# Second feed-forward product: seven block products over 14 of 22 row chunks instead of 12, with three plain chunks ahead instead of four

## The chip, the cores and the metric

The kernel runs on one core of a Trainium2 chip, as one program. The time is the device time of one execution in microseconds (us). The core's engines each work through a queue of their own: TensorE (PE, with its weight loads PEld), VectorE (DVE), ScalarE (ACT), GpSimd (POOL) and SyncE (SP), which here only issues DMAs. Semaphores make one wait for another.

## The reference

Two layers, each of a feed-forward block, a token mixer with three kinds of attention, and another feed-forward block, each with a residual and a layer norm. Four feed-forward blocks in all; the change lies in their second product, `h @ w2`:

```python
D_MODEL = 1024
SEQ = 512
D_FF = 2816

def _swiglu(x, w1, w2):
    gt, up = jnp.split(x @ w1, 2, axis=-1)
    return (jax.nn.silu(gt) * up) @ w2

    for l in range(DEPTH):
        x = _layer_norm(DN_ALPHA * x + 0.5 * _swiglu(x, ffn1_w1[l], ffn1_w2[l]), ln1_g[l], ln1_b[l])
        mix = _token_mix(x, ...)
        x = _layer_norm(DN_ALPHA * x + mix, ln2_g[l], ln2_b[l])
        x = _layer_norm(DN_ALPHA * x + 0.5 * _swiglu(x, ffn2_w1[l], ffn2_w2[l]), ln3_g[l], ln3_b[l])
```

## The kernel before

All matrices are float32 in memory. For TensorE each operand is split into a high part (`hi`, the value rounded to fp32r) and a low part (`lo`, the rest), and each product is made as three: hi x hi, lo x hi, hi x lo. ScalarE makes `hi` (L160 for weights, L434 for activations, L560 for the rows of h), VectorE makes `lo` (L161, L435, L561).

`h` has 2816 rows, 22 chunks of 128 (`KF`). It lies transposed in `ha` (chunks 0 to 17) and `hb` (the tail, 18 to 21, `NTAIL`). Its 512 columns are the tokens. `w2` is 22 chunks of 128 rows by 1024 columns. The result fills eight banks `accs[tb][hf]`: four blocks of 128 tokens, two halves of 512 columns. A plain chunk is 4 x 2 x 3 = 24 products of 128x128 by 128x512 (L195, `mm_rows`).

The order of one feed-forward block behind the first product (`ffn`, `short_rows`, `rows_ln`):

1. Ahead: the plain chunks of `LEAD` (12 to 15 before). While TensorE is in them, the operands of the next part are made.
2. The block part (`short_rows`, products at L453): chunks 0 to 11 (`2 * NW`, NW = 6) are taken as a 2 x 2 block matrix: tokens in halves H1 and H2, chunks in halves of NW, columns in halves of 512. Seven block products (Winograd's form of Strassen's scheme) stand in for eight. The names of the seven, in order of use: f_e (with differences of `bt` and `b1`), f_z (steps `z`), f_1 (with `b1`), f_6 (with `bt`), f_r (steps `r_`), f_7 (with `b1`) and f_4 (with `bt`). Each runs in steps `q` of two chunks: 2 x 2 x 3 = 12 products. `c11` to `c22` are the four quarters of the result in PSUM; `c21` serves as the scratch quarter, and `copies` (L459) and `add` (L464) carry what is shared between the seven.
3. Behind: chunks 16 and 17, plain, then the tail, token block by token block, with the layer norm.

The operands of the block part are made on the way. VectorE makes the block sums of h in `ha` (L477, L482, L483, L507), the differences of w2's quarters in `bt` and `b1` (L490, L497, L517, L537) and all low parts. The split activations lie in four sets of 2 x NW chunks: `xh`, `xl` (the input of the first product, done with by then) and two tiles `fs0`, `fs1`. f_e, f_1, f_z, f_6, f_7, f_r and f_4 take the sets 0, 1, 2, 3, 0, 1, 3. The split weights (`unit`) go round five pairs of buffers, so the split for one step waits for the products of the step five before.

`b1` and `bt` are loaded at the second chunk of `LEAD` (L428); the quarters for `z` and `r_` come through the ring of three `raw` buffers. In the first block of the first layer `b_parts` also paces 16 small loads of GpSimd, one behind each of the first 16 splits (L442, L443).

PE's and POOL's instructions are issued as written. Those of DVE, ACT and SP are put in order by the framework's planner when the program is built, by its own model of time; on the chip each engine then follows that order strictly, and `tc.issue_after` (`behind`) adds edges to it.

The tiles of the pool `stp` lie where the pool `w1p` of the first product was, and wait tile by tile for its last users; behind them the same place goes to `xa` and the tail's `hs` tiles.

Of the kernel before, what the change touches and what calls it, by code (L numbers as in the profile page):

```python
# [66 lines left out]
def body(tc, a, out, depth=DEPTH):  # L67
# [259 lines left out]
    NW = 6  # L327
    LEAD = range(2 * NW, KF - NTAIL - 2)
# [79 lines left out]
    def short_rows(st, w2, accs, hs, h_parts):  # L408
# [5 lines left out]
        pl.tile([P, 2, S], F32R, name="hs", tag="hs", bufs=2)  # L414
        ec, xc = ([pl.tile([P, S], F32, name=f"{n}{t}") for t in range(2)] for n in ("ec", "xc"))
        b1 = [pl.tile([P, KD, P], F32, name=f"b1{q}") for q in range(NW // 2)]
        sets = [x.rearrange("p a (b c) -> p (a b) c", b=2) for x in (xh, xl)]
        sets.append(pl.tile([P, 2 * NW, 256], F32R, name="fs0"))
        pl.tile([P, S], F32, name="uc", tag="uc", bufs=4)
        bt = [pl.tile([P, KD, P], F32, name=f"bt{q}") for q in range(NW // 2)]  # L420
        sets.append(pl.tile([P, 2 * NW, 256], F32R, name="fs1"))
# [4 lines left out]
        def rows(t, r, half, q):  # L426
            k0 = (r * NW + 2 * q) * P
            nc.sync.dma_start(t.rearrange("p (c k) f -> p c (k f)", c=2),  # L428
                              w2[k0:k0 + 2 * P, 512 * half:512 * half + 512].rearrange("(c p) f -> p c f", p=P))
            return t  # L430

        def a_parts(i, src):
            t = sets[i][:, 0:2 * NW]
            A.activation(t[:, 0:NW], src, AF.Copy)  # L434
            tt(t[:, NW:2 * NW], src, t[:, 0:NW].bitcast(F32), op=OP.subtract)  # L435
            return t

        def b_parts(raw):
            w = wsplit(raw)
# [6 lines left out]
        def prod(o, x, w, q, first=False):  # L446
            hi, lo = w
            xh_, xl_ = x[:, 0:NW], x[:, NW:2 * NW]
            for t in range(2):
                for j in range(2):  # L450
                    k, c, s = 2 * q + j, slice(4 * j, 4 * j + 4), slice(t * P, t * P + P)
# [4 lines left out]
        def copies(o, n=None):  # L456
            d = n or [pl.tile([P, S], F32, name="uc", tag="uc", bufs=4) for _ in range(2)]
            for t in range(2):
                A.activation(d[t], o[t], AF.Copy)  # L459
            return d  # L460
# [5 lines left out]
        Q = range(NW // 2)  # L466

        for n, k in enumerate(LEAD):
            if k not in hs:
                h_parts(k, pl.tile([P, 2, S], F32R, name="hs", tag="hs", bufs=2))  # L470
            w = wrows(w2, k)
            if n == 1:
                for q in Q:
                    rows(b1[q], 0, 0, q)
                    rows(bt[q], 0, 1, q)
                with behind(st.last):
                    tt(a21, a21, a22, op=OP.add)  # L477
                    f_e = a_parts(0, a21)
            if n == 2:
                with behind(st.last):  # L480
                    f_1 = a_parts(1, a11)
                    tt(a21, a21, a11, op=OP.subtract)  # L482
                    tt(a11, a12, a21, op=OP.subtract)  # L483
                    f_z = a_parts(2, a11)
# [3 lines left out]

        for q in Q:
            tt(bt[q], bt[q], b1[q], op=OP.subtract)  # L490
            prod(c21, f_e, b_parts(bt[q]), q, q == 0)
        copies(c21, ec)

        def z(q):
            r = rows(wraw(), 1, 1, q)
            prod(c12, f_z, b_parts(r), q)
            tt(bt[q], r, bt[q], op=OP.subtract)  # L497

        z(0)
        f_6 = a_parts(3, a21)  # L500
        for q in Q:
            prod(c21, f_1, b_parts(b1[q]), q, q == 0)
# [5 lines left out]
        f_7 = a_parts(0, a21)  # L508
        for q in Q:
            prod(c21, f_6, b_parts(bt[q]), q)  # L510
            if q == 0:
                z(2)
        u = copies(c21)
        f_r = a_parts(1, a12)
        f_4 = a_parts(3, a22)
        for q in Q:
            tt(b1[q], bt[q], b1[q], op=OP.subtract)  # L517
        h_parts(LEAD[-1] + 1, st.lnp.tile([P, 2, S], F32R, name="hs", tag="t2"))
        w = {}

        def r_(q):
            r = rows(wraw(), 1, 0, q)
            w[q] = r
            prod(c11, f_r, b_parts(r), q)

# [4 lines left out]
        for q in Q:  # L530
            prod(c21, f_7, b_parts(b1[q]), q)
        u = copies(c21)
        add(c21, xc)
        for q in Q:
            if q < 2:
                r_(q + 1)
            tt(bt[q], w[q], bt[q], op=OP.subtract)  # L537
            prod(c21, f_4, b_parts(bt[q]), q)
# [1147 lines left out]
```

## Time and profile before

| | |
|---|---|
| runs | 2430.63, 2430.72, 2431.18 us; median 2430.72 |
| profiled execution | 2430.75 us, of which the span of instructions 2428.7 |
| busy | PE 2417.4 us (100%), PEld 2178.8, DVE 1945.4 (80%), ACT 1235.0 (51%), POOL 264.4 (11%) |
| DMA | 286.29 MB, mean 118 GB/s |
| granted TensorE clock | 0.999 |

The chain is the sequence of work that ended last, followed back from the last instruction. A row of a timeline reads: start, duration, engine, line, operation, output<-inputs, shape, count, and in brackets the idle time just before it and what ended it. Buffer numbers are left out of names, so `bt` stands for each of the three `bt` tiles. Matmuls are pipelined: the duration of one (389 ns) is longer than the distance from one to the next.

### The profile page before, as it was taken

To read this page: it belongs to the slowest core of one execution; us is meant where nothing else is said; L and a number is where in the kernel's file an instruction comes from. 1 tells how busy PE (TensorE), PEld (TensorE's weight loads), DVE (VectorE), ACT (ScalarE), POOL (GpSimd) and SP (SyncE) were. 2 spreads that over 40 slices of the span, in tenths; PEclk is the share of its full clock that TensorE was granted. 3 is DMA by queue.
4 is the path that set the end of the run, shared out by engine and by line. 5 is a ranking of instruction groups with operands and counts; after the bars stand their busy time and mean duration, and the time that the engine had idled before them with its cause. 6 is when DMAs were issued, how large, how long until landed. Compare 5 with 4: busy or idle time off the path is not lost.

```text
span 2428.7 us, 42375 instructions
## 1 busy us (share of the span) xinstructions
PE 2417.4 (100%) x16257; PEld 2178.8 (90%) x16257; DVE 1945.4 (80%) x3786; ACT 1235.0 (51%) x2273; POOL 264.4 (11%) x472
## 2 busy tenths in 40 slices
PE   9999999999999999999999999999999999999998
PEld 9999888888889899998899998878888898999986
DVE  7997975687688689988789979666777886899795
ACT  4454544577644435445445445355766444445452
POOL 2000511133300000000000000122332000000000
PEclk9999999999999999999999999999999999999999
DMA  6332563533134433332533332645321344333233
GB/s 203 106 110 86 162 210 119 158 92 88 45 104 131 134 104 110 113 105 104 165 108 115 109 124 85 189 138 140 100 76 57 101 139 145 91 105 111 90 115 128
DMA packets 382699, 286.29 MB, mean 118 GB/s; under 512 B 17512, under 2 KB 347640, under 8 KB 382496
## 3 DMA queue, kind: packets, MB, share of 16 engines
q1 hardware_dynamic: 375024, 258.68, 35.9%
q0 software_dynamic: 7472, 24.90, 3.0%
q8 instruction: 128, 2.10, 0.4%
q14 instruction: 75, 0.61, 0.1%
HBM read 256.22 MB, written 17.88 MB: 113 GB/s over the span
## 4 chain that ended last, share of the span: by engine, by line
PE 99%; DMA 0%; DVE 0%; POOL 0%; SPq 0%; issue 0%; POOLq 0%; ACT 0%; DVEq 0%
PE pg L373 22%; PE acc L195 13%; PE pu L373 11%; PE acc L453 9%; PE pj L181 6%; PE pj L183 6%; PE pj L182 6%; PE pv L373 5%; PE brp L182 2%; PE brp L181 2%; PE brp L183 2%; PE sN L1081 2%; PE ptN L1123 1%; PE po L1142 1%; PE po L1029 1%; PE sF L1002 1%
## 5 line engine op out<-in xcount | busy, mean ns | idle before, releaser
L161 DVE TENSOR_TENSOR lo<-raw,hi 128x1024 fp32r<-128x1024 f32 x280 | 342.2, 1225 | 121.6 <-ACT hi L160 121.3
L160 ACT ACTIVATE hi<-raw 128x1024 fp32r<-128x1024 f32 x280 | 294.5, 1055 | 228.5 <-PE pg L373 56.9
L373 PE MATMUL pg<-xh,lo 128*128 128x256 f32 x1104 | 312.4, 283 | 0.0
L373 PE MATMUL pg<-xl,hi 128*128 128x256 f32 x1104 | 312.4, 283 | 0.0
L373 PE MATMUL pg<-xh,hi 128*128 128x256 f32 x1104 | 312.3, 283 | 0.0
L181 PE MATMUL pj<-xh,hi 128*128 128x512 f32 (+1 forms) x720 | 267.2, 371 | 0.5 <-ACT hi L1512 0.5
L355 ACT ACTIVATE hi<-ws 128x1024 fp32r<-128x1024 f32 x184 | 191.6, 1055 | 128.3 <-DVE ws L351 63.3
L183 PE MATMUL pj<-xh,lo 128*128 128x512 f32 (+1 forms) x720 | 254.6, 354 | 0.0
L182 PE MATMUL pj<-xl,hi 128*128 128x512 f32 (+1 forms) x720 | 254.4, 353 | 0.0
L356 DVE TENSOR_TENSOR lo<-ws,hi 128x1024 fp32r<-128x1024 f32 x184 | 223.4, 1221 | 38.3 <-ACT hi L355 37.5
L373 PEld LDWEIGHTS pg<-xh,hi 128*128 128x128 f32 x1104 | 211.9, 192 | 0.8
L373 PEld LDWEIGHTS pg<-xl,hi 128*128 128x128 f32 x1104 | 211.9, 192 | 0.8
L373 PEld LDWEIGHTS pg<-xh,lo 128*128 128x128 f32 x1104 | 211.9, 192 | 0.0
L373 PE MATMUL pu<-th,hi 128*128 128x256 f32 x608 | 172.1, 283 | 0.0
L373 PE MATMUL pu<-tl,hi 128*128 128x256 f32 x608 | 172.1, 283 | 0.0
L373 PE MATMUL pu<-th,lo 128*128 128x256 f32 x608 | 172.1, 283 | 0.0
L195 PE MATMUL acc<-hi,hs 128*128 128x512 f32 x512 | 158.2, 390 | 0.0
L183 PEld LDWEIGHTS pj<-xh,lo 128*128 128x128 f32 x720 | 136.1, 189 | 19.9 <-DVE lo L1513 0.2
L181 PEld LDWEIGHTS pj<-xh,hi 128*128 128x128 f32 x720 | 136.4, 189 | 15.5 <-issue 3.1
L358 ACT ACTIVATE dh<-raw 128x512 fp32r<-128x512 f32 x92 | 58.0, 631 | 177.5 <-PE pv L373 116.6
L182 PEld LDWEIGHTS pj<-xl,hi 128*128 128x128 f32 x720 | 136.8, 190 | 11.5 <-DVE xl L1598 0.2
L373 PEld LDWEIGHTS pu<-th,hi 128*128 128x128 f32 x608 | 116.7, 192 | 0.0
(394 smaller groups left out, 6501.5 us busy)
## 6 DMA issues: line engine op xcount, KB each, us to landing
raw<-in_ffn_w_dram SPq DMA_DIRECT2D x240, 512.0 KB, 3.8
raw<-in_w_in_dram SPq DMA_DIRECT2D x56, 512.0 KB, 3.8
raw<-in_w_gate_dram SPq DMA_DIRECT2D x48, 512.0 KB, 3.8
x_sp<-xa POOLq DMA_DIRECT2D x24, 512.0 KB, 5.8
ks<-hl SPq DMA_DIRECT2D x96, 128.0 KB, 2.3
xa<-x_sp POOLq DMA_DIRECT2D x16, 512.0 KB, 7.0
raw<-in_w_out_dram SPq DMA_DIRECT2D x16, 512.0 KB, 3.6
b<-in_ffn_w_dram SPq DMA_DIRECT2D x12, 512.0 KB, 7.6
```

The costliest lines, as they stand in the source:

```text
L160: nc.scalar.activation(hi[:, c], raw[:, c], AF.Copy)
L161: nc.vector.tensor_tensor(lo[:, c], raw[:, c], hi[:, c].bitcast(F32), op=OP.subtract)
L181: nc.tensor.matmul(o, hi[:, k], vh, start=first, stop=False)
L182: nc.tensor.matmul(o, hi[:, k], vl, start=False, stop=False)
L183: nc.tensor.matmul(o, lo[:, k], vh, start=False, stop=last)
L195: nc.tensor.matmul(o, x(k)[:, t], y[:, c], start=first and i == 0, stop=last and i == 2, skip_group_check=True)
L355: pa = nc.scalar.activation(hi, x, AF.Copy)
L356: pv = tt(lo, x, hi.bitcast(F32), op=OP.subtract)
L358: nc.scalar.activation(ud[0], ru[:, h2], AF.Copy)
L373: nc.tensor.matmul(o, wx, vx, start=first and k == 0 and i == 0, stop=k == 3 and i == 2, skip_group_check=True)
L453: nc.tensor.matmul(o[t], u[:, k, s], v[:, c], start=first and j == 0 and i == 0, stop=False, skip_group_check=True)
L1081: nc.tensor.matmul(o[:, 0:nb].rearrange("p k b j -> p (k b j)"), q, kx[:, 2 * b0:2 * (b0 + nb)].rearrange("p a b -> p (a b)"), start=i == ...
```

## The change

NW becomes 7: chunks 0 to 13 go through the seven block products. Each product has 7 chunks and runs in four steps, three pairs and a single (`Q`); loads, splits and differences of the single step are half as large. `LEAD` becomes chunks 14, 15 and 16; behind the block part stands chunk 17 alone. The steps `z` and `r_` become four each and are spread over the loops. For room, `hs` in the pool falls from two buffers to one, `uc` from four to two, and the four sets are taken strictly in turn (f_4 now in set 2, so behind f_z rather than f_6); the two tiles of sets lie directly behind `b1` and `bt`.

The core of the diff:

```diff
         return pts
 
     NTAIL = 4
-    NW = 6
-    LEAD = range(2 * NW, KF - NTAIL - 2)
+    NW = 7
+    LEAD = range(2 * NW, KF - NTAIL - 1)
     PLAIN = (0, 1, 2)
 
     def ffn_first(w1):
@@ -411,32 +411,38 @@
 
         V, A, tt = nc.vector, nc.scalar, nc.vector.tensor_tensor
         pl = pool("stp", side="right", reuse_waits="tile")
-        pl.tile([P, 2, S], F32R, name="hs", tag="hs", bufs=2)
+        pl.tile([P, 2, S], F32R, name="hs", tag="hs")
         ec, xc = ([pl.tile([P, S], F32, name=f"{n}{t}") for t in range(2)] for n in ("ec", "xc"))
-        b1 = [pl.tile([P, KD, P], F32, name=f"b1{q}") for q in range(NW // 2)]
-        sets = [x.rearrange("p a (b c) -> p (a b) c", b=2) for x in (xh, xl)]
-        sets.append(pl.tile([P, 2 * NW, 256], F32R, name="fs0"))
-        pl.tile([P, S], F32, name="uc", tag="uc", bufs=4)
-        bt = [pl.tile([P, KD, P], F32, name=f"bt{q}") for q in range(NW // 2)]
-        sets.append(pl.tile([P, 2 * NW, 256], F32R, name="fs1"))
+        pl.tile([P, S], F32, name="uc", tag="uc", bufs=2)
+        Q = [range(q, min(q + 2, NW)) for q in range(0, NW, 2)]
+        b1, bt = [], []
+        for x, n in ((b1, "b1"), (bt, "bt")):
+            x += [pl.tile([P, 4 * len(q), P], F32, name=f"{n}{q[0]}") for q in Q]
+            pl.tile([P, 2 * NW, 256], F32R, name=f"fs{n}", tag=f"fs{n}")
+        sets = [x.rearrange("p a (b c) -> p (a b) c", b=2)[:, 0:2 * NW] for x in (xh, xl)]
+        nset = [0]
         c11, c12, c21, c22 = ([accs[i + t][j] for t in range(2)] for i in (0, 2) for j in range(2))
         a11, a12, a21, a22 = (st.ha[:, j:j + NW, i] for i in (H1, H2) for j in (0, NW))
         w = {}
 
         def rows(t, r, half, q):
-            k0 = (r * NW + 2 * q) * P
-            nc.sync.dma_start(t.rearrange("p (c k) f -> p c (k f)", c=2),
-                              w2[k0:k0 + 2 * P, 512 * half:512 * half + 512].rearrange("(c p) f -> p c f", p=P))
+            k0, n = (r * NW + q[0]) * P, len(q)
+            t = t[:, 0:4 * n]
+            nc.sync.dma_start(t.rearrange("p (c k) f -> p c (k f)", c=n),
+                              w2[k0:k0 + n * P, 512 * half:512 * half + 512].rearrange("(c p) f -> p c f", p=P))
             return t
 
-        def a_parts(i, src):
-            t = sets[i][:, 0:2 * NW]
+        def a_parts(src):
+            i = nset[0] % 4
+            nset[0] += 1
+            n = (None, None, "b1", "bt")[i]
+            t = pl.tile([P, 2 * NW, 256], F32R, name=f"fs{n}", tag=f"fs{n}") if n else sets[i]
             A.activation(t[:, 0:NW], src, AF.Copy)
             tt(t[:, NW:2 * NW], src, t[:, 0:NW].bitcast(F32), op=OP.subtract)
             return t
 
         def b_parts(raw):
-            w = wsplit(raw)
+            w = wsplit(raw, raw.shape[1])
             if after:
                 i, h = after.pop(0)
                 nc.gpsimd.tensor_copy(pace, w[1][:, 0, 0:1].bitcast(F32))
@@ -447,14 +453,14 @@
             hi, lo = w
             xh_, xl_ = x[:, 0:NW], x[:, NW:2 * NW]
             for t in range(2):
-                for j in range(2):
-                    k, c, s = 2 * q + j, slice(4 * j, 4 * j + 4), slice(t * P, t * P + P)
+                for j, k in enumerate(q):
+                    c, s = slice(4 * j, 4 * j + 4), slice(t * P, t * P + P)
                     for i, (u, v) in enumerate(((xh_, hi), (xl_, hi), (xh_, lo))):
                         nc.tensor.matmul(o[t], u[:, k, s], v[:, c], start=first and j == 0 and i == 0, stop=False,
                                          skip_group_check=True)
 
         def copies(o, n=None):
-            d = n or [pl.tile([P, S], F32, name="uc", tag="uc", bufs=4) for _ in range(2)]
+            d = n or [pl.tile([P, S], F32, name="uc", tag="uc", bufs=2) for _ in range(2)]
             for t in range(2):
                 A.activation(d[t], o[t], AF.Copy)
             return d
@@ -463,79 +469,75 @@
             for t in range(2):
                 tt(o[t], o[t], x[t], op=OP.add)
 
-        Q = range(NW // 2)
-
         for n, k in enumerate(LEAD):
             if k not in hs:
-                h_parts(k, pl.tile([P, 2, S], F32R, name="hs", tag="hs", bufs=2))
+                h_parts(k, pl.tile([P, 2, S], F32R, name="hs", tag="hs"))
             w = wrows(w2, k)
             if n == 1:
-                for q in Q:
-                    rows(b1[q], 0, 0, q)
-                    rows(bt[q], 0, 1, q)
+                for i, q in enumerate(Q):
+                    rows(b1[i], 0, 0, q)
+                    rows(bt[i], 0, 1, q)
                 with behind(st.last):
                     tt(a21, a21, a22, op=OP.add)
-                    f_e = a_parts(0, a21)
+                    f_e = a_parts(a21)
             if n == 2:
                 with behind(st.last):
-                    f_1 = a_parts(1, a11)
+                    f_1 = a_parts(a11)
                     tt(a21, a21, a11, op=OP.subtract)
                     tt(a11, a12, a21, op=OP.subtract)
-                    f_z = a_parts(2, a11)
+                    f_z = a_parts(a11)
             for tb in (2, 3, 0, 1) if n == len(LEAD) - 1 else range(NB):
                 mm_rows(accs, lambda k: hs[k][:, 0], lambda k: hs[k][:, 1], k, tb, w, n == 0, False)
         copies(c21, xc)
 
-        for q in Q:
-            tt(bt[q], bt[q], b1[q], op=OP.subtract)
-            prod(c21, f_e, b_parts(bt[q]), q, q == 0)
+        for i, q in enumerate(Q):
+            tt(bt[i], bt[i], b1[i], op=OP.subtract)
+            prod(c21, f_e, b_parts(bt[i]), q, i == 0)
         copies(c21, ec)
-
-        def z(q):
-            r = rows(wraw(), 1, 1, q)
-            prod(c12, f_z, b_parts(r), q)
-            tt(bt[q], r, bt[q], op=OP.subtract)
+        raws = {}
+
+        def z(i):
+            r = rows(wraw(), 1, 1, Q[i])
+            prod(c12, f_z, b_parts(r), Q[i])
+            tt(bt[i], r, bt[i], op=OP.subtract)
+
+        def r_(i):
+            raws[i] = rows(wraw(), 1, 0, Q[i])
+            prod(c11, f_r, b_parts(raws[i]), Q[i])
 
         z(0)
-        f_6 = a_parts(3, a21)
-        for q in Q:
-            prod(c21, f_1, b_parts(b1[q]), q, q == 0)
+        f_6 = a_parts(a21)
+        for i, q in enumerate(Q):
+            prod(c21, f_1, b_parts(b1[i]), q, i == 0)
         u = copies(c21)
         add(c22, ec)
         z(1)
         add(c11, u)
         tt(a21, a22, a21, op=OP.subtract)
-        f_7 = a_parts(0, a21)
-        for q in Q:
-            prod(c21, f_6, b_parts(bt[q]), q)
-            if q == 0:
-                z(2)
+        f_7 = a_parts(a21)
+        for i, q in enumerate(Q):
+            prod(c21, f_6, b_parts(bt[i]), q)
+            if i + 2 < len(Q):
+                z(i + 2)
         u = copies(c21)
-        f_r = a_parts(1, a12)
-        f_4 = a_parts(3, a22)
-        for q in Q:
-            tt(b1[q], bt[q], b1[q], op=OP.subtract)
+        f_r = a_parts(a12)
+        f_4 = a_parts(a22)
+        for x, y in zip(b1, bt):
+            tt(x, y, x, op=OP.subtract)
         h_parts(LEAD[-1] + 1, st.lnp.tile([P, 2, S], F32R, name="hs", tag="t2"))
-        w = {}
-
-        def r_(q):
-            r = rows(wraw(), 1, 0, q)
-            w[q] = r
-            prod(c11, f_r, b_parts(r), q)
-
         r_(0)
         for t in range(2):
             tt(u[t], u[t], ec[t], op=OP.add)
         add(c12, u)
-        for q in Q:
-            prod(c21, f_7, b_parts(b1[q]), q)
+        for i, q in enumerate(Q):
+            prod(c21, f_7, b_parts(b1[i]), q)
         u = copies(c21)
         add(c21, xc)
-        for q in Q:
-            if q < 2:
-                r_(q + 1)
-            tt(bt[q], w[q], bt[q], op=OP.subtract)
-            prod(c21, f_4, b_parts(bt[q]), q)
+        for i, q in enumerate(Q):
+            if i + 1 < len(Q):
+                r_(i + 1)
+            tt(bt[i], raws[i], bt[i], op=OP.subtract)
+            prod(c21, f_4, b_parts(bt[i]), q)
         add(c22, u)
         pl.tile([P, 88], F32, name="pad")
         pl.release()
```

## Prediction

> **What bounds the kernel now.** I read the page first (span, engines, the chain that ended last), then the chain in order of time around the second feed-forward product, then the stretches of that product by engine, then VectorE's timeline there.
>
> ```profile
> span 2428.7 us, 42375 instructions
> ...
> PE 2417.4 (100%) x16257; PEld 2178.8 (90%) x16257; DVE 1945.4 (80%) x3786; ACT 1235.0 (51%) x2273; POOL 264.4 (11%) x472
> ...
> PE 99%; DMA 0%; DVE 0%; POOL 0%; SPq 0%; issue 0%; POOLq 0%; ACT 0%; DVEq 0%
> ```
>
> The chain is TensorE from end to end. Whatever removes a product shortens the span, as long as the next operand is there in time. The fourth feed-forward stage in the chain in order of time (start, length, what):
>
> ```profile
> 2307.61 21.79 PE acc L195 x96
> 2329.40 57.12 PE acc L453 x252
> 2386.52 32.65 PE acc L195 x144
> ```
>
> 96 products are the four plain chunks ahead (24 each), 252 the seven block products over 12 chunks, 144 the two plain chunks behind and the four of the tail. A product takes 57.12 / 252 = 0.2267 us. No piece stands between them: TensorE waits for nothing here. But it isn't alone in being full. The stretches view (us, then the busy time of PE, PEld, DVE, ACT, POOL with counts, granted clock, DMA share, GB/s):
>
> ```profile
> 2310.42:2376.40 65.98, 65.98 (x293) 54.63 (x292) 65.98 (x61) 38.22 (x41) 0.54 (x1) 1.00 0.35 118
> ```
>
> From 2310.42 to 2376.40 VectorE is busy 65.98 of 65.98 us, as TensorE is; ScalarE 38.22. In this stretch VectorE makes the low half of every operand (L161 of the weights, L435 of the activations) and the sums of blocks. It keeps up, with no slack in its own time, so what counts is how far ahead of its user each result is. VectorE's timeline at the head of that stretch (start, duration, what):
>
> ```profile
> 2310.42 1.75 DVE L477 TENSOR_TENSOR ha<-ha 128x1536 f32<-128x1536 f32 x1
> ...
> 2313.75 1.89 DVE L561 TENSOR_TENSOR hs<-ha,hs 128x512 fp32r<-128x512 f32 x3
> 2315.56 1.75 DVE L435 TENSOR_TENSOR xh<-ha,xh 128x1536 fp32r<-128x1536 f32 x1
> 2317.23 2.38 DVE L490 TENSOR_TENSOR bt<-bt,b 128x1024 f32<-128x1024 f32 x2
> 2319.53 1.75 DVE L482 TENSOR_TENSOR ha<-ha 128x1536 f32<-128x1536 f32 x1
> 2321.20 1.22 DVE L161 TENSOR_TENSOR lo<-raw,hi 128x1024 fp32r<-128x1024 f32 x1
> ...
> 2327.41 1.75 DVE L435 TENSOR_TENSOR fs<-ha,fs 128x1536 fp32r<-128x1536 f32 x1
> 2329.07 1.22 DVE L497 TENSOR_TENSOR bt<-raw,bt 128x1024 f32<-128x1024 f32 x1
> ...
> 2333.62 1.75 DVE L435 TENSOR_TENSOR fs<-ha,fs 128x1536 fp32r<-128x1536 f32 x1
> 2335.29 1.75 DVE L507 TENSOR_TENSOR ha<-ha 128x1536 f32<-128x1536 f32 x1
> 2336.95 1.22 DVE L161 TENSOR_TENSOR lo<-b,hi 128x1024 fp32r<-128x1024 f32 x1
> ```
>
> From start to start a 1536-wide operation takes 1.67 us (2333.62 to 2335.29), a 512-wide one 1.81 / 3 = 0.60 (L561 x3, 2313.75 to 2315.56), and a 1024-wide one 1.14 ((2319.53 - 2317.23) / 2 = 1.15). So 1792 wide is about 1.67 + (1.67 - 1.14) / 2 = 1.93, 0.27 more than now.
>
> The last row is the tightest: the low half of the first pair of b1 for f_1, ready at 2336.95 + 1.22 = 2338.17. Its first user, in TensorE's timeline, and the same pair of rows in the other three stages:
>
> ```profile
> 2340.57 0.39 PE L453 MATMUL acc<-lo,xl 128*128 128x512 f32 x1
> ```
> ```profile
> 270.05 1.22 DVE L161 TENSOR_TENSOR lo<-b,hi 128x1024 fp32r<-128x1024 f32 x1
> ...
> 1133.45 1.22 DVE L161 TENSOR_TENSOR lo<-b,hi 128x1024 fp32r<-128x1024 f32 x1
> ...
> 1474.23 1.22 DVE L161 TENSOR_TENSOR lo<-b,hi 128x1024 fp32r<-128x1024 f32 x1
> ```
> ```profile
> 272.95 0.39 PE L453 MATMUL acc<-lo,xl 128*128 128x512 f32 x1
> ...
> 1136.51 0.39 PE L453 MATMUL acc<-lo,xl 128*128 128x512 f32 x1
> ...
> 1477.05 0.39 PE L453 MATMUL acc<-lo,xl 128*128 128x512 f32 x1
> ```
>
> Spare time: 1.68, 1.84, 1.60 and 2.40 us, 1.88 on the mean. That is all VectorE has in hand at this point.
>
> **The change part by part.** TensorE. Per stage now: 4 x 24 + 252 + 2 x 24 = 396 products before the tail. After: 3 x 24 + 7 x 42 + 24 = 390. Six fewer in each of four stages: 24 x 0.2267 = 5.44 us off the chain. That is 0.22% of the run, hardly more than the 0.2% that a measurement of this kernel can tell from no change.
>
> VectorE up to the tightest point. From 2310.42 it now does eight 1536-wide operations (L477, L482, L483, L507, and L435 for f_1, f_e, f_6 and f_z: 13.4 us), eleven 1024-wide ones (12.5) and three 512-wide (1.8): 27.7 us, and 2310.42 + 27.7 = 2338.1, the time above. After: the eight get 0.27 wider (+2.1); the odd step adds a half difference (L490) and a half split (+2 x 0.60); the fourth chunk ahead takes away its split (-1.14) and its h low half (-0.60). Together +1.6 us.
>
> The time it has. TensorE reaches the first step of f_1 earlier by a whole chunk (24 x 0.2267 = 5.44) less the odd step of f_e (6 x 0.2267 = 1.36): 4.08 us earlier. The chunk that leaves the head comes off the cover of VectorE's work, since the two plain chunks behind become one and the product moves into the block part.
>
> So the split is late by 4.08 + 1.6 - 1.88 = 3.8 us, if VectorE keeps its order. Whether the delay falls at f_1, or a step sooner at f_e or f_z, is the planner's matter; it is one backlog and is paid once per stage. Behind that point VectorE gets 9 more half operations and three wider ones, 9 x 0.60 + 3 x 0.27 = 6.2 us, and TensorE's products last 6 x 1.36 = 8.2 us longer (six odd steps), so nothing further piles up. At the end there is spare now:
>
> ```profile
> 2374.07 1.21 DVE L161 TENSOR_TENSOR lo<-bt,hi 128x1024 fp32r<-128x1024 f32 x1
> ...
> 2392.86 1.23 DVE L161 TENSOR_TENSOR lo<-raw,hi 128x1024 fp32r<-128x1024 f32 x1 [1.21 <-ACT hi L160]
> ```
>
> The last block split is ready at 2375.28 for a step that starts at 2386.52 - 2.72 = 2383.80.
>
> In-order issue makes a late input cost more than itself. In the first stage VectorE waits for a load though L482 behind it needs nothing from it:
>
> ```profile
> 251.47 1.23 DVE L490 TENSOR_TENSOR bt<-bt,b 128x1024 f32<-128x1024 f32 x1 [0.64 <-DMA bt<-in_ffn_w_dram]
> 252.62 1.75 DVE L482 TENSOR_TENSOR ha<-ha 128x1536 f32<-128x1536 f32 x1
> ```
>
> DMA and SP: the bytes of w2 stay the same. b1 and bt become eight loads (two of 256 KB) where there were six, so two more issues on SP's queue ahead of the later raw rows, and the same for the odd z and r rows. Cost 0: the raw rows are covered by VectorE's backlog. If a bt load is exposed it costs what stands above, 0.64 a stage, 2.6 in all; that is in the range.
>
> ScalarE: seven half casts and eleven wider ones against two plain casts less; it is 38.22 of 65.98 us busy. Cost 0; without that cover, one cast (1055 ns by the page's groups) per stage:
>
> ```profile
> L160 ACT ACTIVATE hi<-raw 128x1024 fp32r<-128x1024 f32 x280 | 294.5, 1055 | 228.5 <-PE pg L373 56.9
> ```
>
> Buffers. uc falls from four to two: the third copy into uc must wait for the add that reads the second. Now that add's second half starts at 2371.13 and the copy at 2373.70, so there are 1.9 us between:
>
> ```profile
> 2371.13 0.69 DVE L464 TENSOR_TENSOR acc<-acc,uc 128x512 f32<-128x512 f32 x1
> ```
> ```profile
> 2373.70 0.57 ACT L459 ACTIVATE uc<-acc 128x512 f32<-128x512 f32 x1
> 2387.82 2.17 ACT L560 ACTIVATE hs<-hb 128x512 fp32r<-128x512 f32 x4
> ```
>
> Cost 0, at most 1 us a stage if VectorE is late there too. f_4 now lies where the tail's hs tiles come, so they wait for its last product; the second row shows that they are made behind 2386.52 already. Cost 0. One plain chunk behind instead of two: the tail's last split is ready at 2394.09, 7.6 us behind the products, and waits for the buffer of the first plain chunk (5.44 us). That buffer is then an odd step's, free at once, so it comes about 2.2 behind, for a use at 5.44 or later. Cost 0.
>
> GpSimd, first stage only: 16 small copies pace bvec's loads and each holds a low half. One of them:
>
> ```profile
> 287.72 10.35 POOL L442 COPY pace<-lo 128x1 f32<-128x1 f32 x1
> ```
>
> ```profile
> 297.35 0.68 DVE L528 TENSOR_TENSOR uc<-uc,ec 128x512 f32<-128x512 f32 x1
> 298.10 1.23 DVE L161 TENSOR_TENSOR lo<-raw,hi 128x1024 fp32r<-128x1024 f32 x1
> ```
>
> A split of VectorE starts at 298.10, at once behind that copy; by the pace of 0.60 it could have started at 297.95, so it lost 0.15 us. With 28 splits the buffers come round sooner; from nothing to 16 x 0.15 = 2.4 us. I take 0.2 us and leave it out of the sum.
>
> Sum: -5.44 + 4 x 3.8 = +9.8 us. The profiled execution took 2430.75 us (its span and 2.05 around it), 0.03 from the median of the runs: 2430.75 + 9.8 = 2440.5.
>
> **The rivals.** (a) *Faster: the planner puts the due ones first.* L507, the low half of f_6, two L497 and one h low half stand ahead of the tightest split and are needed only later: 1.93 + 1.93 + 2 x 1.14 + 0.60 = 6.7 us, more than the 3.8 missing. From 3.8 us on of these moved behind, nothing waits: 2430.75 - 5.44 = 2425.3. For it: the order is planned anew. Against it: in the old order these stand ahead too, in all four stages, with 1.6 to 2.4 us in hand, and each stands about where its input came ready, not where it is due.
>
> (b) *Half of it:* the order moves some, and 0.15 to 2.6 us a stage remain: 2425.9 to 2435.7, no change that can be told. At 1.36 us a stage the change is worth exactly nothing.
>
> (c) *The wait slows the clock.* The granted clock is 1.00 in the stretch. At the start of the run it isn't yet:
>
> ```profile
> 1.11 3.78 PE L1494 MATMUL warm<-xl 128*128 128x128 f32 x16 [1.11 <-DVE xl L1489]
> ...
> 5.92 1.06 PE L1494 MATMUL warm<-xl 128*128 128x128 f32 x8
> ```
>
> The same product took 3.78 / 16 = 0.236 us, then 1.06 / 8 = 0.133. If a wait of 3.8 us in one piece brought that back for as long again, it would cost about 1.7 us more (3.8 x (1 - 0.133 / 0.236)) per stage: 2447. Against it: the delay may come in pieces. The Trainium skill has this rule (TensorE: Matmul & The Clock Gate, "HAM oscillation — how this bites in real kernels"): idle gaps of TensorE over about 3.4 us put it back to half its clock. By that page the estimate is a further 3.4 / 2 = 1.7 us a stage for a single gap and none for two smaller ones. No wait in this trace is long enough to show it.
>
> (d) *Longer still:* one more wide operation (1.93) lands ahead of the split: 3.8 + 1.93 = 5.7 us a stage, 2430.75 - 5.44 + 22.9 = 2448.2. The upper end.
>
> **How the numbers follow.** The forecast, a backlog of more than 2.6 us a stage, 0.57; (a) 0.15; (b) 0.20; (c) 0.08. (d) is the upper edge of the first. So faster 0.15, same 0.20, slower 0.65. The range goes from (a) to (d): 2425.0 to 2448.5. The likeliest case's own range is 2436 to 2448.
>
> **What would show it.** In the chain the pieces ahead and of L453 should read x72 and x294 per stage. If I am right, TensorE waits for VectorE (L161 or L435) at the first steps of L453, some 15 us in all, and from the first plain chunk to the last block product a stage takes 72 x 0.2267 + 294 x 0.2267 + 3.8 = 86.8 us against 78.9. By (a) it takes 83.0 and VectorE's L507 and L497 stand behind the splits of f_1. By (c) the clock column falls below 1.00 behind the wait. The prediction is wrong if the order changes as in (a), or if VectorE finds work of the block part to do before 2310.42, where it still idles:
>
> ```profile
> 2302.43 0.69 DVE L561 TENSOR_TENSOR hi<-ha,hi 128x512 fp32r<-128x512 f32 x1 [3.07 <-ACT hi L560]
> ```

## The result, and the profile after

| | before | after |
|---|---|---|
| median of 6 runs | 2431.04 us | 2450.69 us |
| span of the profiled execution | 2428.7 us | 2450.3 us |
| granted TensorE clock | 0.999 | 0.997 |

The ratio is 1.0084, 95% interval 1.0071 to 1.0097: 19.65 us slower. The six products fewer per stage should give 5.44 us, so the change lost 25.1 us, 6.3 per stage, where 3.8 were forecast: the direction was right, the size was not, and the time lies 2 us above the forecast's upper end. Line numbers of after differ from those of before: L441 is the low half of an activation set, L459 the block products, L470 the adds into the result, L494, L502, L526 and L539 the differences of w2, L481, L486, L487 and L516 the block sums.

The page of after, span, engines and the chain that ended last:

```profile
span 2450.3 us, 42417 instructions
...
PE 2421.5 (99%) x16233; PEld 2175.9 (89%) x16233; DVE 1972.0 (80%) x3814; ACT 1244.0 (51%) x2285; POOL 272.8 (11%) x472
...
PE 92%; DVE 4%; DMA 2%; issue 1%; SPq 0%; ACT 0%; POOL 0%; DVEq 0%; POOLq 0%; ACTq 0%
```

TensorE's share of the chain fell from 99% to 92%, and VectorE and a DMA are in it. The waits of the weight loads in after (who waited for what: us in all, times, longest):

```profile
PEld acc L459 <- DVE lo L161: 17.6, 12, 2.4
...
PEld acc L459 <- DVE fsb L441: 5.6, 4, 2.2
...
PEld acc L195 <- DVE hs L563: 1.5, 2, 1.2
```

Together 24.7 of the 25.1 us that are missing. The places in the fourth stage, from the timeline of the weight loads (in brackets the idle time before):

```profile
2344.74 0.19 PEld L459 LDWEIGHTS acc<-lo,xh 128*128 128x128 f32 x1 [1.32 <-DVE lo L161]
...
2349.75 0.19 PEld L459 LDWEIGHTS acc<-lo,xh 128*128 128x128 f32 x1 [2.42 <-DVE lo L161]
...
2355.70 0.19 PEld L459 LDWEIGHTS acc<-hi,fsb 128*128 128x128 f32 x1 [2.22 <-DVE fsb L441]
...
2368.78 0.19 PEld L459 LDWEIGHTS acc<-lo,fsb 128*128 128x128 f32 x1 [0.75 <-DVE lo L161]
```

These are the second and the third step of f_e, the first step of f_z and the step z(1). None is at the first split of f_1, where the prediction looked for the tightest point. What VectorE did up to there (timeline of after):

```profile
2333.31 1.23 DVE L494 TENSOR_TENSOR bt<-bt,b 128x1024 f32<-128x1024 f32 x1 [1.02 <-DMA bt<-in_ffn_w_dram]
...
2337.53 1.22 DVE L161 TENSOR_TENSOR lo<-bt,hi 128x1024 fp32r<-128x1024 f32 x1
2338.66 2.02 DVE L486 TENSOR_TENSOR ha<-ha 128x1792 f32<-128x1792 f32 x1
2340.59 1.22 DVE L494 TENSOR_TENSOR bt<-bt,b 128x1024 f32<-128x1024 f32 x1
2341.73 1.22 DVE L502 TENSOR_TENSOR bt<-raw,bt 128x1024 f32<-128x1024 f32 x1
2342.86 0.69 DVE L494 TENSOR_TENSOR bt<-bt,b 128x512 f32<-128x512 f32 x1
2343.47 1.22 DVE L161 TENSOR_TENSOR lo<-bt,hi 128x1024 fp32r<-128x1024 f32 x1
2344.60 2.02 DVE L487 TENSOR_TENSOR ha<-ha 128x1792 f32<-128x1792 f32 x1
2346.54 2.02 DVE L441 TENSOR_TENSOR fsbt<-ha,fsbt 128x1792 fp32r<-128x1792 f32 x1
2348.47 1.82 DVE L161 TENSOR_TENSOR lo<-bt,hi 128x1024 fp32r<-128x1024 f32 x2
```

The second split of f_e stands at 2343.47, behind L502 (an operand of f_6), L486 and two later differences; the third at 2348.47, behind f_6's low half at 2346.54, which TensorE first touches at 2370.99, 22 us after it is ready. From 2337.53 on VectorE is never idle in these rows; part of what it does first is due much later.

### The profile page after: what moved, and what is told of

Same layout as the page of the kernel before. It is cut to its first block, busy times and chain, and to the rows that moved or that the text cites. A ratio compares the mean times of both kernels' runs of the same rounds, so it can differ in the third digit from the quotient of the medians.

```text
span 2450.3 us, 42417 instructions
## 1 busy us (share of the span) xinstructions
PE 2421.5 (99%) x16233; PEld 2175.9 (89%) x16233; DVE 1972.0 (80%) x3814; ACT 1244.0 (51%) x2285; POOL 272.8 (11%) x472
## 4 chain that ended last, share of the span: by engine, by line
PE 92%; DVE 4%; DMA 2%; issue 1%; SPq 0%; ACT 0%; POOL 0%; DVEq 0%; POOLq 0%; ACTq 0%
PE pg L373 21%; PE pu L373 11%; PE acc L195 8%; PE acc L459 8%; PE pj L181 6%; PE pj L182 6%; PE pj L183 6%; PE pv L373 5%; PE brp L182 2%; PE brp L181 2%; PE brp L183 2%; PE sN L1083 2%; PE ptN L1125 1%; PE po L1144 1%; DVE lo L161 1%
## 5 line engine op out<-in xcount | busy, mean ns | idle before, releaser
L161 DVE TENSOR_TENSOR lo<-raw,hi 128x1024 fp32r<-128x1024 f32 (+1 forms) x280 | 338.7, 1212 | 123.9 <-ACT hi L160 122.7
L160 ACT ACTIVATE hi<-raw 128x1024 fp32r<-128x1024 f32 (+1 forms) x280 | 291.5, 1044 | 229.2 <-PE pg L373 56.6
L356 DVE TENSOR_TENSOR lo<-ws,hi 128x1024 fp32r<-128x1024 f32 x184 | 223.5, 1222 | 37.2 <-ACT hi L355 36.7
L195 PE MATMUL acc<-hi,hs 128*128 128x512 f32 x384 | 119.4, 391 | 0.8 <-DVE hs L563 0.8
```

The costliest lines, as they stand in the source:

```text
L160: nc.scalar.activation(hi[:, c], raw[:, c], AF.Copy)
L161: nc.vector.tensor_tensor(lo[:, c], raw[:, c], hi[:, c].bitcast(F32), op=OP.subtract)
L195: nc.tensor.matmul(o, x(k)[:, t], y[:, c], start=first and i == 0, stop=last and i == 2, skip_group_check=True)
L356: pv = tt(lo, x, hi.bitcast(F32), op=OP.subtract)
```

## The experiments

The theories: *order* (there is enough time, but VectorE's queue holds work due later ahead of the next split) against *amount* (too much work for the time, whatever the order), and beside them the *cover* (the lead chunk that was taken away). Every kernel was timed against the kernel before on the same chip. "Missing" is the median less 2425.3, the time of before without the products that fall away.

| run | us | ratio to before, 95% | missing |
|---|---|---|---|
| after | 2450.69 | 1.0071 to 1.0097 | 25.4 |
| due order, no interleaving | 2476.76 | 1.0172 to 1.0206 | 51.5 |
| f_6 alone moved | 2449.07 | 1.0058 to 1.0088 | 23.8 |
| before, three ahead | 2448.57 | 1.0056 to 1.0086 | (17.4 above before) |
| after, four ahead | 2450.98 | 1.0067 to 1.0097 | 25.7 |
| due order, head only | 2451.52 | 1.0067 to 1.0100 | 26.2 |
| due order to f_6's end | 2453.29 | 1.0070 to 1.0103 | 28.0 |
| less VectorE work | 2471.86 | 1.0155 to 1.0189 | 46.6 |
| due order throughout, VectorE alone | 2461.98 | 1.0112 to 1.0143 | 36.7 |
| due order, both engines | 2433.45 | 0.9998 to 1.0016 | 8.2 |
| the same, tail held back | 2459.46 | 1.0098 to 1.0131 | 34.2 |
| the same, raw rows freed early | 2426.45 | 0.9971 to 0.9989 | 1.2 |

**The cover alone.** In the kernel before:

```diff
-    LEAD = range(2 * NW, KF - NTAIL - 2)
+    LEAD = range(2 * NW, KF - NTAIL - 3)
```

> The kernel before (twelve chunks by block products) with three plain chunks ahead and three behind in place of four and two: the cover alone, no wider work. By the prediction's sum: 5.44 us less time, 1.74 less work, 1.88 in hand, so 1.8 us late per stage: 2438 us. If the whole loss comes from the lost chunk of cover: 2450 us or more. If cover isn't what counts: 2431 us.

2448.57: 17.4 us slower, 4.4 per stage, not 1.8. Only the cover changed here. So the other part, the wider operations and the odd step, costs (2450.69 - 2448.57 + 5.44) / 4 = 1.9 us a stage; the prediction's sum gives 3.8 - 1.8 = 2.0 for that. This is a difference of two kernels that were each ordered anew, so the two parts need not simply add up. The mis-sized term is the cover. Its waits in the fourth stage, with VectorE's rows ahead of them (timelines of this run):

```profile
2337.07 1.22 DVE L490 TENSOR_TENSOR bt<-bt,b 128x1024 f32<-128x1024 f32 x1
2338.20 1.22 DVE L161 TENSOR_TENSOR lo<-raw,hi 128x1024 fp32r<-128x1024 f32 x1
2339.34 1.75 DVE L435 TENSOR_TENSOR fs<-ha,fs 128x1536 fp32r<-128x1536 f32 x1
2341.01 1.22 DVE L497 TENSOR_TENSOR bt<-raw,bt 128x1024 f32<-128x1024 f32 x1
2342.14 1.22 DVE L161 TENSOR_TENSOR lo<-bt,hi 128x1024 fp32r<-128x1024 f32 x1
```
```profile
2343.41 0.19 PEld L453 LDWEIGHTS acc<-lo,xh 128*128 128x128 f32 x1 [3.01 <-DVE lo L161]
...
2347.35 0.19 PEld L453 LDWEIGHTS acc<-lo,xh 128*128 128x128 f32 x1 [1.34 <-DVE lo L161]
```

3.01 + 1.34 = 4.35, about the loss of this stage. In the other three the wait at the second step is as long (3.0 to 3.1 us) and of the second wait at most 0.3 is left; there the granted clock fell behind the first wait (0.54 from 1130.45 to 1134.00, but 1.00 from 2343.41 to 2347.00), and the slower products took the time instead. The same split in the kernel before:

```profile
2323.47 1.22 DVE L490 TENSOR_TENSOR bt<-bt,b 128x1024 f32<-128x1024 f32 x1
2324.60 1.22 DVE L161 TENSOR_TENSOR lo<-bt,hi 128x1024 fp32r<-128x1024 f32 x1
2325.74 1.75 DVE L483 TENSOR_TENSOR ha<-ha 128x1536 f32<-128x1536 f32 x1
```

There it is ready at 2325.82 for a product at 2329.40 + 14 x 0.2267 = 2332.57: 6.75 us in hand, and L483, f_z's low half and L497 come behind it. With one chunk less the planner put those three and z(0)'s split ahead of it. The order isn't a constant that a cover is taken from; it is made anew, and a split that had 6.75 us in hand became the late one. That the new order, and not the amount of work, sets the price is read from these rows; a run in due order was made for the changed kernel only.

**Cover given back.** After with `LEAD = range(2 * NW, KF - NTAIL)` (14 to 17, none behind), the fourth chunk's `hs` in the place of `t2`.

> The changed kernel with all four plain chunks ahead of the block part and none behind it: cover given back, the wider work kept. By the prediction's sum: 3.3 us more work, 1.36 more time, 1.88 in hand, 0.1 us late per stage: 2425.5 us. Order theory: part of the waits stays, since f_6, L502 and L516 still stand ahead of splits: 2427 to 2435 us. If the cover were beside the point: 2450 us.

2450.98, but the waits are elsewhere (this run's waits of the weight loads):

```profile
PEld acc L195 <- ACT hs L561: 12.1, 4, 3.2
...
PEld acc L195 <- DVE hs L562: 4.6, 4, 1.2
...
PEld acc L459 <- DVE lo L161: 3.7, 7, 1.3
```

In the block part 3.7 us are left of 23.2. The 16.7 at L195 are the first tail chunk, for which nothing was ready because no plain chunk stands behind the block part any more. So with four ahead 0.9 us a stage is left in the block part, where the sum gives 0.1; the run says nothing for the total, since the edit made a wait of its own, with a clock that fell behind it (0.87 to 0.94 on the mean in the four tails).

**One operation moved.**

```diff
-        f_6 = a_parts(a21)
...
         z(1)
+        with behind(lnq.lo):
+            f_6 = a_parts(a21)
```

`lnq.lo` is here the low half of z(1)'s split.

> The changed kernel with one thing moved: cast and low half of f_6 come behind the split of z(1); nothing else is held. Order theory: one operation of 1.93 us comes out from ahead of the splits of f_e, so up to 1.9 us a stage less, 2443 to 2447 us, with what else is early (L502, L516, L526) still in the way. Amount theory: 2450 to 2452 us, the delay only shows somewhere else.

2449.07: the waits at f_e fell, and the wait for f_z's low half rose, from 5.6 to 13.4 us in all:

```profile
PEld acc L459 <- DVE fsb L441: 13.4, 4, 3.4
PEld acc L459 <- DVE lo L161: 6.4, 8, 1.5
```

By itself this run looks like *amount*: what is taken out at one step is missing at the next. But other early work had moved up: three L502 and a split of f_1 now stand ahead of f_z's low half, where after has two L502, that split and f_6's low half.

**All of it in due order, first try.** VectorE's operations are linked in the order of their use, each difference directly ahead of its own split:

```diff
+        def tt(*x, **kw):
+            with behind(link[0]):
+                i = V.tensor_tensor(*x, **kw)
+            if link[1]:
+                link[0] = i.ins
...
+                tt(a21, a21, a22, op=OP.add)
+                f_1 = a_parts(a11, 1)
+                f_e = a_parts(a21, 0)
...
         for i, q in enumerate(Q):
             tt(bt[i], bt[i], b1[i], op=OP.subtract)
             prod(c21, f_e, b_parts(bt[i]), q, i == 0)
+            if i == 1:
+                tt(a21, a21, a11, op=OP.subtract)
+                tt(a11, a12, a21, op=OP.subtract)
+        f_z = a_parts(a11, 2)
```

> The changed kernel with the same instructions, but VectorE's queue in the block part is held in the order in which TensorE needs the results: the next split first, f_z before f_6, L516, f_7, L502 and L526 only behind the splits of f_1 and z(1). Order theory (there is time enough, but operations that are due later stand ahead): the waits of TensorE go, 2450.7 - 25 = 2425 to 2429 us. Amount theory (the prediction's: 3.8 us of work per stage too much by then, in any order): at least 2440 us, with the wait at the splits of f_1.

2476.76, far worse, for a reason of its own (VectorE's timeline of this run; L416 are the linked operations):

```profile
2351.17 1.22 DVE L416 TENSOR_TENSOR bt<-bt,b 128x1024 f32<-128x1024 f32 x1
2353.57 1.23 DVE L161 TENSOR_TENSOR lo<-bt,hi 128x1024 fp32r<-128x1024 f32 x1 [1.17 <-ACT hi L160]
```

A split needs ScalarE's cast of the difference just ahead of it, so VectorE stood 1.17 us at this pair, and 1.13 at the next. The run doesn't decide between the theories. An order has to be due and also leave a cast's time between a result and its use.

**Due order with interleaving, in three steps.** Each run carries the linked order on: first up to the splits of f_1, then to the last step of f_6 and the splits of f_7, then to the end. The core of the first (`go` puts its operation behind the last linked one; in these runs the linked sums and differences are L451, splits' low halves still L161, the adds L479 and the products L468):

```diff
+        diff(0)
+        diff(1)
+        go(two, a21, a21, a11, OP.subtract)
+        w = [go(b_parts, bt[0])]
+        diff(2)
+        w.append(go(b_parts, bt[1]))
+        go(two, a11, a12, a21, OP.subtract)
+        diff(3)
+        w += [go(b_parts, bt[i]) for i in (2, 3)]
+        f_z = go(a_parts, a11)
         for i, q in enumerate(Q):
-            tt(bt[i], bt[i], b1[i], op=OP.subtract)
-            prod(c21, f_e, b_parts(bt[i]), q, i == 0)
+            prod(c21, f_e, w[i], q, i == 0)
```

> The changed kernel with the same instructions; VectorE's queue is held in due order up to the splits of f_1 as in the first run, but interleaved, so that no operation stands directly behind the difference whose cast it needs: differences 0 and 1 and L486 before the first split of f_e, each later difference or block sum one place ahead of its split, the low half of f_z before the splits of z(0) and f_1; f_6, L502, L516, f_7, L526 and the low half for the tail are only held behind those splits, in no fixed order. Order theory: worked out from the trace of after with these durations every split is there 1.5 us or more ahead of its user, so no waits of TensorE are left: 2425 to 2428 us, and the first run was slow because VectorE waited for ScalarE's casts (1.1 to 2.1 us at each pair). Amount theory: the same 3.8 us or more a stage are still missing: 2440 us or more.

2451.52. In the fourth stage the waits of 1.3, 2.4 and 2.2 us at f_e and f_z became 0.63 and 0.36, and a new one came at the first split of f_6:

```profile
2368.79 0.28 PEld L468 LDWEIGHTS acc<-lo,fsbt 128*128 128x128 f32 x1 [3.93 <-DVE lo L161]
```

Ahead of that split stood a block sum, two differences for f_7 and the h low half of the plain chunk behind, none of them linked.

> As the run before (VectorE's queue held in due order), carried on to the end of the block part: the splits of z(1), f_6, z(2), z(3) and f_7 are linked too, and L516, f_7, f_r, f_4, the differences for f_7 and f_4, the tail's low half and the adds into the sums come behind the splits that TensorE needs first. At the head L486 comes ahead of difference 1 (its load came 1.74 us late for that place), and difference 3 ahead of L487. Order theory: the wait of 3.9 us at the first split of f_6 had the same cause as those before (L516, two differences for f_7 and a low half for the tail stood ahead of it) and goes without a successor: 2425 to 2430 us. Amount theory: the missing time comes back at a later step: 2440 us or more.

2453.29. The chain in order of time, fourth stage, shows 132 products of the block part in 29.90 us, as many times 0.2267: no wait from f_e to z(2).

```profile
2325.56 16.35 PE acc L195 x72
2341.91 29.90 PE acc L468 x132
```

The time came back behind it, at the add of xc (L479) ahead of f_4 (14.1 us in all) and at a split of f_7 (6.3):

```profile
PEld acc L468 <- DVE acc L479: 14.1, 4, 3.7
PEld acc L468 <- DVE lo L161: 6.3, 4, 1.8
```

> The same instructions on the same engines as the changed kernel; VectorE's queue is held in due order through the whole block part, the tail of it too (each difference for f_7 just ahead of its split, the two adds of xc ahead of the later splits of f_4, the tail's low half and the adds of u into c22 last). In the run before VectorE was busy almost without a gap from 2328.4 to 2402.8 while the block part ended 7.4 us late of what its products take, because the add of xc (3.0 us) and a split of f_7 (1.1 us) stood behind work due later. By the order theory the work fits, with 1 us or more in hand at every step: 2425 to 2430 us. By the amount theory (VectorE has more to do than the block part lasts) 2440 us or more, with a wait at a new place.

2461.98. VectorE's queue was now in due order to the end, and the next engine's wasn't (VectorE's and ScalarE's timelines of this run):

```profile
2392.66 1.23 DVE L161 TENSOR_TENSOR lo<-b,hi 128x1024 fp32r<-128x1024 f32 x1 [3.62 <-ACT hi L160]
```
```profile
2390.62 1.06 ACT L160 ACTIVATE hi<-raw 128x1024 fp32r<-128x1024 f32 x1 [1.89 <-PE acc L468]
2391.59 1.04 ACT L160 ACTIVATE hi<-b 128x1024 fp32r<-128x1024 f32 x1
```

ScalarE waited with the cast of a raw row for a buffer that TensorE still used, and the cast that VectorE needed stood behind it.

**Both queues.**

```diff
+        def part(raw):
+            with behind(cast[0]):
+                r = go(b_parts, raw)
+            cast[0] = lnq.hi
+            return r
...
+        w = part(bt[0])
+        with behind(cast[0]):
+            u = copies(c21)
+        add_to(c21, xc)
+        prod(c21, f_4, w, Q[0])
```

`cast[0]` is ScalarE's last linked cast.

> The same instructions as the changed kernel. The head of the block part as in the run that had no wait of TensorE over its first 132 products; behind it each difference for f_7 stands two places ahead of its split, the adds of xc come directly behind the first split of f_4 and ahead of its later ones, and from f_r on ScalarE's casts are held in the same order too (in the last run a cast of a raw row that waited for its buffer stood ahead of a cast that VectorE needed, 3.6 us). Order theory: with VectorE's and ScalarE's queues both in due order the waits of 1.1 and 3.0 us at the end go as well: 2425 to 2429 us, 0.1 to 0.2% below the kernel before. Amount theory: VectorE has been busy without a gap up to here, so what is taken out at one step is missing at the next: 2440 us or more.

2433.45, interval 0.9998 to 1.0016 of before: 17.2 of the 25.4 us are back, by order alone. The run also moves the differences for f_7 and the adds of xc in VectorE's queue, so ScalarE's share of this is not told apart. What is left: 2.2 us at the add of xc (four times, the longest 0.7) and waits behind the block part.

> As the run before, with three places changed: the first difference for f_4 ahead of f_4's low half (so that ScalarE's cast of it runs beside that), the second behind the adds of xc; the adds of u into c22 ahead of the last split of f_4; the split of the plain chunk behind the block part held behind that one. Order theory: the last wait in the block part (0.5 to 0.7 us a stage for the add of xc) goes, 2.2 us in all, and the layer norm's waits behind the block part (4 us in all, from the loads that wait for the block part's buffers) get smaller: 2426 to 2431 us. If those 8 us that are left over 2425.3 are the amount (VectorE ends its block work too late for the tail, whichever way it is sorted), 2433 us as before.

2459.46, a miss. The block part ran without a wait, but the tail's rows were loaded late: ScalarE waited 2.92, 4.67 and 3.92 us for them in the fourth stage, and the loads waited for `raw` buffers that the differences for f_4 still read (SyncE's waits for these, L172 <- bt L451: 50.9 us in all, 35.0 in the run before and 34.8 in the next). Three places were moved at once, so what each of them cost is not shown. The waits of the weight loads in this run:

```profile
PEld acc L195 <- ACT hi L160: 20.2, 8, 3.8
```

The last run holds the cast of that one plain chunk alone and frees the buffers early, directly behind the split of each row; the adds of u into c22 move to the end (the core, against the run before):

```diff
                 prod(c11, f_r, r_part(i + 1), Q[i + 1])
+                for_4(i + 1)
             prod(c21, f_4, part(bt[i]), Q[i])
-            for_4(i + 1)
```

> As the run before, but the differences for f_4, which hold the buffers of the raw rows, come directly behind the splits of those rows, and the plain chunk behind the block part is held behind the last split of f_4 in ScalarE's queue alone. In the run before the block part ran without a wait, but the tail's raw rows came 3 to 4 us late twice a stage, since their buffers were freed late. Order theory: block part without a wait as there, tail rows early as two runs before: 2425 to 2431 us. If the waits behind the block part stay, VectorE has too little time for the block part and the tail together, and it is 2433 us or more.

2426.45: 0.9980 of before, interval 0.9971 to 0.9989, so 4.8 us faster than before and 24.2 faster than after, with the same work on the same engines. The chain of this run in the first stage, and the stretches view from the first plain chunk ahead to the end of the block part in the fourth (us, busy PE, PEld, DVE, ACT, POOL, granted clock, DMA share, GB/s):

```profile
239.92 16.35 PE acc L195 x72
256.26 66.64 PE acc L468 x294
```
```profile
2304.09:2387.06 82.97, 82.97 (x368) 68.68 (x367) 80.41 (x76) 46.55 (x51) 2.12 (x4) 1.00 0.36 121
```

TensorE is busy 82.97 of 82.97 us, and VectorE 80.41: the work does fit, with 2.6 us to spare. With so little to spare, an operation in the wrong place finds nothing to make up for it.

**Less work for VectorE.** The block sum and the differences for f_7 on GpSimd:

```diff
-        tt(a21, a22, a21, op=OP.subtract)
+        nc.gpsimd.tensor_tensor(a21, a22, a21, op=OP.subtract)
...
-            tt(x, y, x, op=OP.subtract)
+            nc.gpsimd.tensor_tensor(x, y, x, op=OP.subtract)
```

> The changed kernel in its own order, but the block sum L516 (1.93 us) and the four differences L526 for f_7 (4.0 us), which are due late and stand ahead of splits, are done by GpSimd: 5.9 us a stage less for VectorE. Order and amount theories agree that this helps where those operations stood ahead (the split of z(1), 0.75 to 0.93 us in two stages); they differ ahead of it: by the order theory the waits at f_e and f_z (5.0 to 6.0 us a stage) stay, since f_6, L502 and the rest still stand in the way there: 2446 to 2449 us. By the amount theory a backlog of 6.3 us a stage less 5.9 leaves almost none: 2425 to 2430 us. If GpSimd's work slows VectorE's, slower than that.

2471.86, slower than after by 21.2 us. GpSimd took far longer for the same operations, and a split of VectorE slowed beside it (GpSimd's and VectorE's timelines, fourth stage; the row x4 holds the four differences, three of 128x1024 and one half as wide):

```profile
2362.60 14.86 POOL L516 TENSOR_TENSOR ha<-ha 128x1792 f32<-128x1792 f32 x1 [246.04 <-DVE fsbt L441]
2377.43 12.49 POOL L526 TENSOR_TENSOR b<-bt,b 128x1024 f32<-128x1024 f32 x4
```
```profile
2382.10 3.38 DVE L161 TENSOR_TENSOR lo<-raw,hi 128x1024 fp32r<-128x1024 f32 x1
```

The block sum took 14.86 us (1.93 on VectorE), the wide differences 2.86, 4.14 and 3.35 us (1.14 on VectorE). So the run doesn't test the amount; the last run does.

## Why the prediction was right in direction and wrong in size

*TensorE, 5.44 us off the chain: right.* The last run has the pieces x72 and x294 and is 4.8 us below before.

*The cover: the step that failed.* "So the split is late by 4.08 + 1.6 - 1.88 = 3.8 us, if VectorE keeps its order. Whether the delay falls at f_1, or a step sooner at f_e or f_z, is the planner's matter; it is one backlog and is paid once per stage." VectorE didn't keep its order, and the price depends on it. The 1.88 us in hand were those of one split in one order. With the shorter cover the operations around f_e were sorted anew and a split that had 6.75 us in hand came last. The run with three chunks ahead puts the cover at 4.4 us a stage where the same sum gives 1.8; the width came to 1.9 where it gives 2.0. The sum also credited 1.74 us for the split and the low half of the fourth chunk. Those lie ahead of the first difference, which waits for its load (1.02 us in the rows above), so part of that credit only made VectorE idle, just ahead of the unbroken row of work in which the late splits stand; how much that cost was not tested alone.

*"nothing further piles up" behind f_1: wrong.* In after z(1) waits 0.75 us in the fourth stage. When the head was put right the wait came at f_6, then at the add of xc and f_7. VectorE has 2.6 us to spare over 83 in the last run; the comparison of 6.2 us more work with 8.2 more time was a balance of totals and held no bound on any one step.

*Rival (a), the due ones first, 2425.3 us, chance 0.15: its mechanism and price were right (2426.45), its condition wasn't met.* The planner doesn't do it by itself. The argument against it, that operations stand where their inputs come ready, is what after shows. To move f_1's and f_6's early operations was not enough, though, as its text had it ("From 3.8 us on of these moved behind, nothing waits"): the runs that came back to before's time had the whole block part in due order, and ScalarE's casts from f_r on.

*Rival (b):* not seen; after's loss was 6.3 us a stage. *Rival (d), 2448.2:* nearest, one more wide operation ahead of the split; f_6's low half is that operation at the third step of f_e. But moving it away gave back 1.6 us in all, not the 7.7 that (d) counts for it, so that (d) comes near is in part luck.

*Rival (c), the clock: it was in after, at the third step of f_e, but added nothing to the total.* That wait is 2.4 us long in every stage. Behind it the clock fell in the first and the third stage (0.50 and 0.54 for some 3 us) and stayed at 1.00 in the second and the fourth. Where it fell, the wait for f_z that comes next was shorter, 0.6 us instead of 2.2, since VectorE sets the time there; the first stage:

```profile
271.90 0.19 PEld L459 LDWEIGHTS acc<-hi,fsb 128*128 128x128 f32 x1 [0.62 <-DVE fsb L441]
```

These two stages lost 5.7 and 5.9 us, the others 6.8 and 6.2. The price of (c) was met in the experiments, below.

*Costs put at nothing.* ScalarE: no block product waited for it in after, but with VectorE's queue alone in due order one of its casts held VectorE up for 3.62 us. uc: no wait. b and bt loads: VectorE waited 1.02 us for the first in the fourth stage, and with due order nothing of that reached TensorE. f_4's set and the tail's `hs`: 1.5 us in all at L195. The pacing copies of GpSimd: the first stage lost no more than the others (88.71 us from 241.18 to 329.89, 82.97 without waits).

## What to carry to other kernels

When an engine's queue is ordered by a planner, time in hand read off one trace belongs to that order; take away cover and the queue is sorted anew, so price the change by the total work against the total time, and by what will stand ahead of each next use. Here an engine that is 97% busy beside the bound needed its queue in order of use, with a cast's time between a result and its reader and with the engine that feeds it in the same order. Where one place only was mended, the wait moved to the next: up to the run with both queues the best step gave back 1.6 us of 25, and most of them lost time.

## What the runs showed of the hardware

*The clock can halve behind a wait of TensorE, and the length of the wait alone doesn't decide it.* In the run with less VectorE work, TensorE waited 3.13 us by its timeline, and products behind it went at 0.43 us instead of 0.23 (the chain has x196 in 47.52 us there, in after in 44.76). The stretches view (granted clock is the third value from the end):

```profile
2385.50:2389.00 3.50, 3.47 (x8) 2.79 (x9) 3.50 (x2) 0.56 (x1) 3.50 (x2) 0.50 0.45 150
```

But in after a wait of 1.99 us was enough in the first stage and one of 2.00 us was not in the fourth, and of two waits of 3.5 us in the run with the head alone in due order, the one in the second stage left the clock at 1.00 and the one in the fourth didn't (idle times of TensorE; its weight loads show 0.4 us more). Two stretches of after, then two of that run, each behind the wait:

```profile
266.96:270.00 3.04, 3.04 (x9) 2.36 (x8) 3.04 (x4) 0.35 (x1) 3.04 (x1) 0.50 0.06 7
2349.75:2353.25 3.50, 3.50 (x15) 2.92 (x16) 3.50 (x4) 1.12 (x2) 0.00 (x0) 1.00 0.00 0
```
```profile
1155.12:1158.62 3.50, 3.50 (x15) 2.91 (x16) 3.50 (x5) 0.63 (x1) 0.00 (x0) 1.00 0.21 80
2368.80:2372.30 3.50, 3.50 (x9) 2.81 (x10) 3.50 (x5) 0.00 (x0) 0.00 (x0) 0.56 0.20 75
```

Where it falls, it cost 1.8 to 3 us on top of the wait (in the run to f_6's end 15.38 us for x60 instead of 60 x 0.2267 = 13.60, in the run with less VectorE work 47.52 for x196 instead of 44.43), and nothing in after, where the next wait took it up. The Trainium skill (TensorE: Matmul & The Clock Gate, "HAM oscillation — how this bites in real kernels") names idle gaps over about 3.4 us. These traces agree that the clock halves, but not on that length, and the measurement decides: 1.99 us was enough in one place and 3.51 us was not in another. What decides between them stays open.

*GpSimd and VectorE slow each other.* The block sum of 128x1792 took GpSimd 14.86 us in the fourth stage, beside operations of VectorE that mostly kept their 1.22 us; in the first stage it took 4.07 us, and a split of VectorE beside it 5.32. A split beside GpSimd's differences went from 1.22 to 3.38 us. The Trainium skill (SBUF — State Buffer, "Who interferes with whom") says that a VectorE instruction with two inputs in SBUF contends with a GpSimd instruction that reads SBUF, and that the order of issue decides which one blocks. The trace agrees in kind: either engine's operations grew longer, and the timeline shows no wait for a semaphore inside them. The order of issue was not tested.
